# Attention with rope, two heads at a time: 128-row score products first, then the 64-row products of both heads in turns

## The chip, the core and the metric

One core of a Trainium2 chip runs the kernel. The metric is device time in microseconds (us). The kernel before took 2066.39 us, the median of three runs (2065.8 to 2067.51).

## What is computed

Two transformer blocks on 256 tokens of 2048 features, in float32. The first has sliding-window attention. The second has two attentions side by side, one with rope ("mla", 16 heads) and a differential one (8 heads), and a feed-forward layer. The change concerns the attention with rope, whose scores are a sum of two products: over 128 features of a head's own keys, and over 64 turned features whose keys all heads share.

```python
def mla_branch(c_q, c_kv, k_pe, ...):
    q = (rmsnorm_2(c_q, q_norm_g) @ w_uq).reshape(b, s, 16, 192)
    q_nope, q_rope = q[..., :128], apply_rope(q[..., 128:], cos, sin)
    kv = (rmsnorm_2(c_kv, kv_norm_g) @ w_ukv).reshape(b, s, 16, 256)
    k_nope, v = kv[..., :128], kv[..., 128:]
    k_rope = apply_rope(k_pe, cos, sin)                  # one for all heads
    # for each of the two blocks of 128 queries:
    sc = (einsum('bqhd,bkhd->bhqk', qn, k_nope) + einsum('bqhr,bkr->bhqk', qr, k_rope)) * scale
    sc = where(chunk_allowed(q_pos, k_pos), sc, -1e30)   # chunks of 64 tokens
    o = einsum('bhqk,bkhd->bqhd', softmax(sc), v)
```

No key of the second block of 128 is allowed to a query of the first. So a head has two score products: first queries with first keys (128 columns), second queries with all keys (256 columns).

## The kernel before

**Large matrices.** All weights lie in HBM as one run of 128x128 tiles in the order of use. SyncE's queue loads them 16 tiles at a time; half of that (8 tiles) at a time is split into an exact high part (`w_hi`, ScalarE, line 84) and a low part (`w_lo`, VectorE, line 85), with four buffers for each. A product with a tile is two instructions on TensorE, 512 columns with the high part and 256 with the low one, in `tile3`. Sums stand in four PSUM banks tagged `g`; from there ScalarE and VectorE take them (`total`, `scaled`, line 198 for the tensor-tensor operations, line 356 for the copy).

**Small work in between.** Attention is written as generators. `Interleave` (line 123) lets one of them go one step after every `every` tiles of weights, and a step of the same piece comes at the earliest `apart` steps later. In the part of interest `every` is 5 and `apart` is 4 (line 703). A planner then orders each engine's instructions by program order and by when it expects operands and buffers to be free, so that an instruction with a late operand may be passed by later ones.

**Attention with rope.** The loop at line 688 runs over four groups of four heads. A group makes its keys (`uk`, 4 x 4 tiles), its values (`uv`, 16 tiles, four at a time), its rope queries (`uq`, 2 x 6 tiles; two heads to a tile, each in one half of the 128 partitions) and its other queries (4 x 6 tiles). Behind the rope queries `rope_q` is queued, which turns them (`rotate`, line 618), and behind each head's queries `attend_m` (line 660), which waits until its group's queries are turned. Its three steps:
1. The scores into a bank tagged `s` (there are two). `scores` (line 363) does, in this order: 128 rows, 128 columns; 64 rows, 128 columns; 128 rows, 256 columns; 64 rows, 256 columns. All operands are float32, and the trace shows each product as two passes (a weight load and a matmul each). `exps` (line 371) takes the negated maximum on VectorE (line 375) and the exponential and its sum on ScalarE (line 379); the probabilities are then divided by the sum.
2. Three transposes into a bank tagged `t` (two of them), and a copy to SBUF on VectorE.
3. The products with the values, and the split of the result into `y_m`.

**Two other attentions** show in the trace what the change makes of this one. `attend_a` (line 442), in the first block, takes two heads at a time, whose 64 features lie in the two halves of the partitions; its products go in turns on the halves, into two `s` banks. `attend_d` (line 725) has two score sets of 128 rows in one step.

Of the kernel before, what the change touches and what calls it, by code (L numbers as in the profile page):

```python
# [10 lines left out]
F32R = mybir.dt.float32r  # L11
# [21 lines left out]
class Weights:  # L33
    """The weight matrices as one run of 128x128 tiles in the order of their use."""

# [19 lines left out]
    def pin(self, after, until):  # L55
        """Splits of tiles from `after` to `until`, counted from here, keep their place in the program."""
        i = len(self.order)
        self.pinned = range(i + after, i + until)

    def cut(self, i, parts=None):  # L60
        """The exact parts [hi], [lo] of half a chunk."""
        if i in self.halves:
            return
        nc = self.nc
        c = i // CH
        if c not in self.loaded:
            self.load(c)
        o = (i % CH) * P
        src = self.loaded[c][:, o:o + HALF * P]
        if o:  # L70
            self.loaded.pop(c)
        if parts is not None:
            self.halves[i] = parts
            for j, (hi, lo) in enumerate(parts):
                q = slice(j * HALF * P // 2, (j + 1) * HALF * P // 2)
                nc.scalar.copy(out=hi, in_=src[:, q])
                nc.vector.tensor_tensor(out=lo, in0=src[:, q], in1=hi.bitcast(F32), op=ALU.subtract)
            return
        hi = self.split.tile([P, HALF * P], F32R, name="w_hi", tag="w_hi", bufs=4)
        lo = self.split.tile([P, HALF * P], F32R, name="w_lo", tag="w_lo", bufs=4)  # L80
        n_cut = 2 if i < self.fine else 1
        for j in range(n_cut):
            q = slice(j * HALF * P // n_cut, (j + 1) * HALF * P // n_cut)
            a = nc.scalar.copy(out=hi[:, q], in_=src[:, q])  # L84
            b = nc.vector.tensor_tensor(out=lo[:, q], in0=src[:, q], in1=hi.bitcast(F32)[:, q], op=ALU.subtract)  # L85
            if i in self.pinned:
                self.tc.keep_in_program_order(a)
                self.tc.keep_in_program_order(b)
        self.halves[i] = [(hi, lo)]
# [16 lines left out]
class Lazy:  # L106
    """A list whose entries are made when they are first asked for, one ahead."""

# [14 lines left out]
class Interleave:  # L123
    """Pieces of work that go between the products of the large matrices, one step at a time.

    A piece is a generator; what it yields is the number of steps after which it goes on.
    """

# [39 lines left out]
def block_kernel(ctx, tc, order, w, xt, cols, bc, fg, cst, out):  # L168
# [30 lines left out]

# [1 line left out]
    ones = const.tile([P, P], F32, name="ones")  # L201
# [24 lines left out]

# [1 line left out]
    def split_scaled(src, g, hl):  # L228
        """hl = [hi | lo] of src * g, one factor per partition."""
        hi = hl[:, 0:S]  # L230
        if g is None:
            a = nc.scalar.copy(out=hi, in_=src)
            b = nc.vector.tensor_tensor(out=hl[:, S:], in0=src, in1=hi.bitcast(F32), op=ALU.subtract)
        else:
            a = nc.scalar.activation(out=hi, in_=src, func=AF.Copy, scale=g)
            b = nc.vector.scalar_tensor_tensor(out=hl[:, S:], in0=src, scalar=g, in1=hi.bitcast(F32),
                                               op0=ALU.mult, op1=ALU.subtract)
        return a, b

    class Squares:  # L240
        """Sums of squares over the features, for every token."""

# [37 lines left out]
    def rows(r, rb=None):  # L280
        """[any partition, token] = r[token, block], in PSUM, and in rb."""
        dg = unit("diag")[:, 0:S]
        for tb in range(2):
            nc.vector.tensor_scalar(out=dg[:, tb * P:tb * P + P], in0=ident, scalar1=r[:, tb:tb + 1], scalar2=None,  # L284
                                    op0=ALU.mult)
        ps = bank("t")
        mm(ps[:, 0:S], ones, dg, True, True)
        if rb is not None:
            nc.vector.tensor_copy(out=rb, in_=ps[:, 0:S])
        return ps[:, 0:S]  # L290

    def tile3(ps, name, row, col, hl, first, last):
        """One tile of weights against [hi | lo]: the product is the sum of the halves of ps."""
        hi, lo = W.take(name, row, col)
        mm(ps, hi, hl, first, False)
        mm(ps[:, 0:S], lo, hl[:, 0:S], False, last)
        between.tiles(1)

    def gemm(name, m, acts):
        """128 output features, transposed."""  # L300
        ps = bank("g")
# [5 lines left out]
    def gemm4(name, ms, acts):  # L307
        """As gemm, four at a time: for activations that come one by one."""
        pp = [bank("g"), bank("g"), bank("s"), bank("s")]
# [6 lines left out]
    def gemm_sum(name, m, acts):  # L316
        """As gemm, all products in one sum."""
        ps = bank("g")
# [9 lines left out]
    def blocks(name, m0, n, acts):  # L328
        """(block, bank) for n blocks, the first four by contraction."""
        for j, ps in enumerate(gemm4(name, range(m0, m0 + 4), acts)):  # L330
# [4 lines left out]
    def nat3(o, hl, tb, hi, lo, first, last):  # L335
        """Tokens as the stationary operand: o[token, feature]."""
        xh = hl[:, tb * P:tb * P + P]
# [5 lines left out]
    def gemm_nat(name, col, acts):  # L343
        """512 output features with the tokens in partitions: one bank for each block of tokens."""
        pp = [bank("g") for _ in range(2)]
# [8 lines left out]
    def total(o, ps):  # L354
        """The two halves of a product."""
        nc.scalar.copy(out=o, in_=ps[:, S:])
        tt(o, o, ps[:, 0:S], ALU.add)
# [5 lines left out]
    def scores(parts, ps):  # L363
        """ps[:, 0:128]: first queries, first keys; ps[:, 128:384]: second queries, all keys."""
        n = len(parts)
# [5 lines left out]
    def exps(ps, table, scale, negmax, sums, init):  # L371
        """exp(scale * (ps + table) - max) and its sums."""
        t = unit("prob")[:, 0:384]
# [9 lines left out]
    def transposed(p, on_act=False):  # L383
        """[keys, queries] of p: first keys (both blocks of queries), then second keys."""
        ps = bank("t")
# [8 lines left out]

    # ================= first block =================
    sq = Squares(8)
# [45 lines left out]
    def attend_a(j, q, o):  # L442
        """Heads a (an even group of keys) and b (an odd one), in the halves of the partitions."""
        kt = j // 8
# [41 lines left out]
    for j in range(16):  # L486
# [7 lines left out]
        for i, b in ((0, ps_0), (1, ps)) if j == 1 else ((j, ps),):  # L494
# [4 lines left out]
            between.add(attend_a(i, half(q, i), half(o, i)))  # L499
    # lambda, negated, in every partition  # L500
    lam = unit("lam")
# [72 lines left out]

    # ================= second block =================
    rope = unit("rope")
# [41 lines left out]
    def rotate(a):  # L618
        """Rope on a[:, 0:256] in place, both halves of the partitions alike."""
        ps = bank("t")  # L620
# [38 lines left out]

    def attend_m(head, qn, qr, kn, v):  # L660
        while head // 4 not in roped:
            yield
        negmax, sums, rec = sm("negmax"), sm("sums"), sm("rec")
        ps = bank("s")
        rng = slice(64 * (head % 2), 64 * (head % 2) + 64)
        scores([(qn, kn), (qr[rng], kr[rng])], ps)
        p = exps(ps, tab_m, scale_m, negmax, sums, BIG)
        nc.vector.reciprocal(out=rec[:, 0:2], in_=sums[:, 0:2])
        nc.scalar.activation(out=p[:, 0:P], in_=p[:, 0:P], func=AF.Copy, scale=rec[:, 0:1])
        nc.vector.tensor_scalar(out=p[:, P:384], in0=p[:, P:384], scalar1=rec[:, 1:2], scalar2=None, op0=ALU.mult)  # L670
        yield
        pt = transposed(p)
        yield
        ps = bank("t")
        mm(ps[:, 0:S], v[0], pt[:, 0:S], True, False)
        mm(ps[:, P:S], v[1], pt[:, S:384], False, True)
        y_m[head] = unit(f"y_m{head}", F32R)
        split_scaled(ps[:, 0:S], None, y_m[head])

# [8 lines left out]
    for u in range(4):  # L688
# [20 lines left out]
        for i in range(4):  # L709
            ps = gemm("uq", 4 * u + i, cq)  # L710
            if i % 2 == 0:
                qn.append(unit("q_n"))
            scaled(half(qn[-1], i), ps, rb_q)
            between.add(attend_m(4 * u + i, half(qn[-1], i), half(qr, i // 2), half(kn[i // 2], i),
                                 [t[:, i * P:i * P + P] for t in v]))

    # differential attention
    y_d = [None] * 16
# [117 lines left out]

    # residual, feed-forward
    sq = Squares(16)
# [127 lines left out]
def _matrices(i):  # L966
    """The weight matrices, their rows and columns in the order in which the kernel has the features."""
    pairs = []
# [60 lines left out]
```

## Time and profile before

| | |
|---|---|
| time, median of three runs | 2066.39 us |
| profiled execution: span, first to last instruction | 2065.4 us |
| TensorE (PE) busy | 2045.3 us, 99% |
| VectorE (DVE) busy | 1294.0 us, 63% |
| ScalarE (ACT) busy | 1057.7 us, 51% |
| chain that ended last | PE 98% |

The profile gives the profiled execution's own time only as its span; 1.0 us lies between that and the median of the runs. In the rows below, PE is TensorE's matmuls and PEld its weight loads, times are us from the span's start, and "L195" is line 195 (the helper that every matmul goes through, so groups are told apart by tile names: `ps_s<-k_n,q_n` are 128-row score products, `ps_s<-rb_kr,q_r` the 64-row ones). Matmuls overlap: the start of the next one tells more than the duration.

### The profile page before, as it was taken

The numbers are of one execution on the slowest core, as the hardware profiler recorded it, in microseconds if no ns is written. First come the engines' busy times: TensorE is split into PE (matmuls) and PEld (weight loads), VectorE is DVE, ScalarE is ACT, GpSimd is POOL, SyncE is SP. The second block draws the span as 40 slices with busy tenths as digits, with TensorE's granted clock in tenths as the row PEclk, the third lists the DMA queues.
The fourth block names the chain that finished last, engine by engine and source line by source line (L and its number), as shares of the span: only waits on it lengthen the run. The fifth ranks groups of instructions, "written<-read, shape, count | busy, mean of one in ns | idle before, by whom it ended". The sixth has DMA issues, their size and how long they took to land.

```text
span 2065.4 us, 28636 instructions
## 1 busy us (share of the span) xinstructions
PE 2045.3 (99%) x11290; PEld 1745.2 (84%) x11290; DVE 1294.0 (63%) x2145; ACT 1057.7 (51%) x1810; POOL 15.6 (1%) x25
## 2 busy tenths in 40 slices
PE   8999999999999999999999999999999999999998
PEld 7878888888888888888888888888888888888886
DVE  7768766877666555566565667655656555554443
ACT  6667555655545444455464445454444444444443
POOL 0000000000000000000000000000000000000000
PEclk9999999999999999999999999999999999999999
DMA  7433454443434555545545555555555555555552
GB/s 291 147 135 141 165 202 186 147 159 123 146 125 176 184 188 183 184 166 181 180 167 184 184 185 185 182 182 184 184 185 186 191 189 188 184 206 201 185 202 102
DMA packets 53670, 364.92 MB, mean 177 GB/s; under 512 B 6240, under 2 KB 7136, under 8 KB 10400
## 3 DMA queue, kind: packets, MB, share of 16 engines
q1 hardware_dynamic: 52560, 361.07, 48.9%
q8 instruction: 88, 1.44, 0.3%
q0 software_dynamic: 400, 1.31, 0.2%
q10 hardware_dynamic: 576, 0.72, 0.1%
q14 instruction: 46, 0.38, 0.1%
HBM read 360.98 MB, written 2.10 MB: 176 GB/s over the span
## 4 chain that ended last, share of the span: by engine, by line
PE 98%; DVE 1%; issue 0%; ACT 0%; DMA 0%; POOL 0%; SPq 0%; ACTq 0%; POOLq 0%
PE ps_g L195 89%; PE ps_s L195 5%; PE ps_t L195 2%; PE ps_t L387 1%; DVE w_lo L85 0%; DMA w_raw<-w 0%; ACT w_hi L84 0%; DVE prob L375 0%; PE ps_t L768 0%; PE ps_t L864 0%; PE ps_t L744 0%; POOL rstd L277 0%; DVE diag L284 0%; DVE prob L468 0%; DVE y L561 0%
## 5 line engine op out<-in xcount | busy, mean ns | idle before, releaser
L85 DVE TENSOR_TENSOR w_lo<-w_raw,w_hi 128x1024 fp32r<-128x1024 f32 (+1 forms) x676 | 825.2, 1221 | 649.2 <-ACT w_hi L84 644.9
L84 ACT CAST w_hi<-w_raw 128x1024 fp32r<-128x1024 f32 (+1 forms) x676 | 707.5, 1047 | 851.8 <-PE ps_g L195 598.1
L195 PE MATMUL ps_g<-h,w_hi 128*128 128x512 f32 x3064 | 1100.4, 402 | 6.5 <-ACT w_hi L84 6.5
L195 PE MATMUL ps_g<-h,w_lo 128*128 128x256 f32 x3064 | 861.2, 281 | 0.0
L195 PEld LDWEIGHTS ps_g<-h,w_hi 128*128 128x128 f32 x3064 | 576.4, 188 | 152.4 <-issue 7.4
L195 PEld LDWEIGHTS ps_g<-h,w_lo 128*128 128x128 f32 x3064 | 579.5, 189 | 1.4 <-DVE w_lo L85 0.4
L195 PE MATMUL ps_g<-w_hi,act 128*128 128x512 f32 x704 | 217.0, 389 | 0.0
L195 PEld LDWEIGHTS ps_g<-w_hi,act 128*128 128x128 f32 x704 | 132.1, 188 | 27.5
L195 PE MATMUL ps_g<-w_lo,act 128*128 128x512 f32 x352 | 136.9, 389 | 0.0
L195 PE MATMUL ps_g<-y_m,w_hi 128*128 128x512 f32 x256 | 91.4, 399 | 0.0
L195 PE MATMUL ps_g<-y_d,w_hi 128*128 128x512 f32 x256 | 90.5, 399 | 0.0
L195 PE MATMUL ps_g<-g,w_hi 128*128 128x512 f32 (+1 forms) x240 | 80.0, 383 | 0.0
L195 PE MATMUL ps_g<-mg,w_hi 128*128 128x512 f32 x224 | 79.9, 399 | 0.0
L195 PE MATMUL ps_g<-w_hi,h 128*128 128x512 f32 x256 | 79.5, 389 | 0.0
L195 PEld LDWEIGHTS ps_g<-w_lo,act 128*128 128x128 f32 x352 | 66.1, 188 | 13.7
L195 PE MATMUL ps_g<-c,w_hi 128*128 128x512 f32 x208 | 77.3, 410 | 0.0
L195 PE MATMUL ps_g<-y_d,w_lo 128*128 128x256 f32 x256 | 71.9, 281 | 0.0
L195 PE MATMUL ps_g<-y_m,w_lo 128*128 128x256 f32 x256 | 71.8, 281 | 0.0
L379 ACT ACTIVATE prob<-prob,negmax 128x128 f32<-128x128 f32 (+1 forms) x128 | 57.0, 447 | 23.2 <-DVE negmax L375 23.0
L195 PE MATMUL ps_g<-g,w_lo 128*128 128x256 f32 x224 | 63.0, 281 | 0.0
L195 PE MATMUL ps_g<-mg,w_lo 128*128 128x256 f32 x224 | 62.9, 281 | 0.0
L195 PE MATMUL ps_g<-c,w_lo 128*128 128x256 f32 x208 | 58.3, 280 | 0.0
(238 smaller groups left out, 2031.3 us busy)
## 6 DMA issues: line engine op xcount, KB each, us to landing
w_raw<-w SPq DMA_DIRECT2D x337, 1024.0 KB, 4.8
w_raw<-w SPq DMA_DIRECT2D x5, 512.0 KB, 8.2
out<-x2n SPq DMA_DIRECT2D x8, 256.0 KB, 3.1
x_t<-xt SPq DMA_DIRECT2D x7, 256.0 KB, 7.6
fgt<-fg POOLq DMA_DIRECT2D x4, 256.0 KB, 6.5
w_raw<-w SPq DMA_DIRECT2D x2, 256.0 KB, 4.3
x_t<-xt SPq DMA_DIRECT2D x2, 128.0 KB, 3.1
lam<-bc POOLq DMA_DIRECT2D x1, 256.0 KB, 4.7
```

What stands on the lines that cost most here:

```text
L84: a = nc.scalar.copy(out=hi[:, q], in_=src[:, q])
L85: b = nc.vector.tensor_tensor(out=lo[:, q], in0=src[:, q], in1=hi.bitcast(F32)[:, q], op=ALU.subtract)
L195: nc.tensor.matmul(out=o, lhsT=a, rhs=b, start=start, stop=stop, skip_group_check=True)
L379: nc.scalar.activation(out=t[:, a:b], in_=t[:, a:b], func=AF.Exp, scale=-1.0, bias=negmax[:, qb:qb + 1], accum_out=sums[:, qb:qb + 1])
L387: nc.tensor.transpose(out=ps[:, j * P:j * P + P], in_=p[:, j * P:j * P + P], identity=ident)
```

## The change

`attend_m` takes two heads. It asks for both `s` banks, does the 128-row products of the first head, then those of the second, and then the 64-row products: 128 columns of the first head (rows 0 to 63) and of the second (rows 64 to 127), then 256 columns of both. The reciprocal is taken once for a pair. The transposes of both heads are one step, and the copy of the second head's goes to ScalarE. The value products of both heads are one step, into one `t` bank. A pair is queued behind every second head's queries. Comments and docstrings elsewhere are emptied; line numbers stay nearly the same.

```diff
-    def attend_m(head, qn, qr, kn, v):
-        while head // 4 not in roped:
+    def attend_m(j, qn, qr, kn, v):
+
+        while j // 2 not in roped:
             yield
         negmax, sums, rec = sm("negmax"), sm("sums"), sm("rec")
-        ps = bank("s")
-        rng = slice(64 * (head % 2), 64 * (head % 2) + 64)
-        scores([(qn, kn), (qr[rng], kr[rng])], ps)
-        p = exps(ps, tab_m, scale_m, negmax, sums, BIG)
-        nc.vector.reciprocal(out=rec[:, 0:2], in_=sums[:, 0:2])
-        nc.scalar.activation(out=p[:, 0:P], in_=p[:, 0:P], func=AF.Copy, scale=rec[:, 0:1])
-        nc.vector.tensor_scalar(out=p[:, P:384], in0=p[:, P:384], scalar1=rec[:, 1:2], scalar2=None, op0=ALU.mult)
-        yield
-        pt = transposed(p)
+        pp = [bank("s") for _ in range(2)]
+        for e, ps in enumerate(pp):
+            mm(ps[:, 0:P], qn[e][:, 0:P], kn[e][:, 0:P], True, False)
+            mm(ps[:, P:384], qn[e][:, P:S], kn[e], False, False)
+        for a, b, n in ((0, P, P), (P, S, S)):
+            for e, ps in enumerate(pp):
+                rng = slice(64 * e, 64 * e + 64)
+                mm(ps[:, a:a + n], qr[rng, a:b], kr[rng, 0:n], False, a > 0)
+        p = [exps(ps, tab_m, scale_m, negmax[:, 2 * e:2 * e + 2], sums[:, 2 * e:2 * e + 2], BIG)
+             for e, ps in enumerate(pp)]
+        nc.vector.reciprocal(out=rec, in_=sums)
+        for e in range(2):
+            nc.scalar.activation(out=p[e][:, 0:P], in_=p[e][:, 0:P], func=AF.Copy, scale=rec[:, 2 * e:2 * e + 1])
+            nc.vector.tensor_scalar(out=p[e][:, P:384], in0=p[e][:, P:384], scalar1=rec[:, 2 * e + 1:2 * e + 2],
+                                    scalar2=None, op0=ALU.mult)
+        yield
+        pts = [transposed(p[e], e == 1) for e in range(2)]
         yield
         ps = bank("t")
-        mm(ps[:, 0:S], v[0], pt[:, 0:S], True, False)
-        mm(ps[:, P:S], v[1], pt[:, S:384], False, True)
-        y_m[head] = unit(f"y_m{head}", F32R)
-        split_scaled(ps[:, 0:S], None, y_m[head])
+        for e in range(2):
+            o = e * S
+            mm(ps[:, o:o + S], v[e][0], pts[e][:, 0:S], e == 0, False)
+            mm(ps[:, o + P:o + S], v[e][1], pts[e][:, S:384], False, e == 1)
+        for e in range(2):
+            y_m[2 * j + e] = unit(f"y_m{2 * j + e}", F32R)
+            split_scaled(half(ps, e), None, y_m[2 * j + e])
...
-            between.add(attend_m(4 * u + i, half(qn[-1], i), half(qr, i // 2), half(kn[i // 2], i),
-                                 [t[:, i * P:i * P + P] for t in v]))
+            if i % 2:
+                between.add(attend_m(2 * u + i // 2, [half(qn[-1], e) for e in range(2)], half(qr, i // 2),
+                                     [half(kn[i // 2], e) for e in range(2)],
+                                     [[t[:, e * P:e * P + P] for t in v] for e in (i - 1, i)]))
```

## Rows read from the trace of the kernel before

**Rows 1.** The page: span, busy time of the engines, chain that ended last by engine.
```profile
span 2065.4 us, 28636 instructions
PE 2045.3 (99%) x11290; PEld 1745.2 (84%) x11290; DVE 1294.0 (63%) x2145; ACT 1057.7 (51%) x1810; POOL 15.6 (1%) x25
...
PE 98%; DVE 1%; issue 0%; ACT 0%; DMA 0%; POOL 0%; SPq 0%; ACTq 0%; POOLq 0%
```

**Rows 2.** Waits of PE, longest in total first: us, times, longest.
```profile
PE ps_g L195 <- ACT w_hi L84: 6.5, 1, 6.5
```

**Rows 3.** Busy time by stretch: length, engines' busy us (instructions), clock, DMA share, GB/s.
```profile
430.00:616.00 186.00, 186.00 (x988) 151.91 (x987) 129.48 (x292) 94.84 (x195) 0.00 (x0) 1.00 0.39 137
...
447.40:465.00 17.60, 17.60 (x81) 12.61 (x80) 13.85 (x44) 9.52 (x27) 0.00 (x0) 1.00 0.31 120
```

**Rows 4.** Timeline of PE at the first head's scores: start us, us, instruction.
```profile
449.01 0.27 PE L195 MATMUL ps_g<-c,w_lo 128*128 128x256 f32 x1
449.12 0.38 PE L195 MATMUL ps_s<-k_n,q_n 128*128 128x128 f32 x2
...
450.48 0.70 PE L195 MATMUL ps_s<-rb_kr,q_r 64*128 64x256 f32 x2
...
451.44 0.28 PE L195 MATMUL ps_g<-c,w_lo 128*128 128x256 f32 x1
```

**Rows 5.** Timeline of PE at one pair of the first block's attention.
```profile
46.95 0.28 PE L195 MATMUL ps_g<-h,w_lo 128*128 128x256 f32 x1
47.16 0.93 PE L195 MATMUL ps_s<-k_a,q_a 64*128 64x128 f32 x8
...
48.36 0.28 PE L195 MATMUL ps_g<-h,w_lo 128*128 128x256 f32 x1
...
48.72 0.28 PE L195 MATMUL ps_g<-h,w_lo 128*128 128x256 f32 x1
```

**Rows 6.** Score products by tile: count, ns min/median/max, first and last start us.
```profile
L195 PE MATMUL ps_s<-k_n,q_n x64: 270/327/483, 449.1 to 593.7; 128*128 128x128 f32 x32, 128*128 128x256 f32 x32
...
L195 PE MATMUL ps_s<-rb_kr,q_r x64: 272/374/480, 449.4 to 594.3; 64*128 64x128 f32 x32, 64*128 64x256 f32 x32
```

**Rows 7.** Timeline of PE at two score sets of the differential attention.
```profile
638.64 0.28 PE L195 MATMUL ps_g<-h,w_lo 128*128 128x256 f32 x1
638.75 1.47 PE L195 MATMUL ps_s<-qk_d 128*128 128x128 f32 x8
...
640.30 0.28 PE L195 MATMUL ps_g<-h,w_lo 128*128 128x256 f32 x1
```

**Rows 8.** Timeline of PE at another pair of the first block's attention.
```profile
189.83 0.92 PE L195 MATMUL ps_s<-k_a,q_a 64*128 64x128 f32 x4
...
191.11 0.92 PE L195 MATMUL ps_s<-k_a,q_a 64*128 64x128 f32 x4
191.96 0.39 PE L195 MATMUL ps_g<-h,w_lo 128*128 128x256 f32 x1
```

**Rows 9.** Timeline of DVE behind the turning of the first group's queries.
```profile
449.42 0.42 DVE L198 TENSOR_TENSOR q_r<-q_r,rope_t 128x256 f32<-128x256 f32 x1
449.75 0.42 DVE L198 TENSOR_TENSOR q_n<-q_n,rb_lat 128x256 f32<-128x256 f32 x1
```

**Rows 10.** Timeline of all engines behind one pair of the first block.
```profile
80.75 0.93 PE L195 MATMUL ps_s<-k_a,q_a 64*128 64x128 f32 x8
...
81.81 0.35 DVE L375 CUSTOM_DVE_ANT_0 prob<-ps_s,bias,negsink 128x128 f32<-128x128 f32 x1 [2.60 <-ACT w_hi L84]
...
82.49 0.08 DVE L375 DVE_READ_ACCUMULATOR2_ANT negmax<- 128x1 f32 x1
...
83.17 0.08 DVE L375 DVE_READ_ACCUMULATOR2_ANT negmax<- 128x1 f32 x1
...
83.77 1.22 DVE L85 TENSOR_TENSOR w_lo<-w_raw,w_hi 128x1024 fp32r<-128x1024 f32 x1
...
85.69 0.70 ACT L467 ACTIVATE prob<-prob,rec 128x128 f32<-128x128 f32 x2
```

## Prediction

> **What bounds the kernel now.** I read the page first: span, busy line, chain. TensorE is busy for 99% of the span and the chain that ended last runs over it for 98% [rows 1]. The list of its waits is the second view: one wait of 6.5 us, for the first weights, is the longest [rows 2]. So a microsecond taken from TensorE's queue comes off the span, unless something else is then late. The third view is the busy time by stretch: in the attention with rope (430 to 616 us) TensorE is busy for all 186 us, VectorE for 129.48, ScalarE for 94.84, and the clock is granted in full [rows 3]. Where the scores of the first four heads lie (447.4 to 465) VectorE is busy for 13.85 of 17.6 us; it is the engine to watch.
>
> The time of before in the runs is 2066.39 us; the profiled execution has a span of 2065.4, so 1.0 us lies around it. The sum is made on the span and carried over.
>
> **What it removes: the switches.** Between large products TensorE does one head's scores: a 128-row product of 128 columns, a 64-row one, a 128-row one of 256 columns, a 64-row one, each in two passes. The timeline shows what a head takes [rows 4]: from the start of the last weight product before it (449.01) to the start of the first such product behind the next large one (451.44) are 2.43 us. Without a head, one such step of a large product takes 0.35 us (48.36 to 48.72 is 0.36 [rows 5]). A head so costs 2.08 us, and a pair, with no switch saved between its two heads, 4.16. There are 64 passes of either kind [rows 6], that is 16 heads with four of each, or eight pairs.
>
> **What it adds.** The new order does both heads' 128-row products, then the four 64-row products in turns on the halves of the rows. Both parts stand in the trace of before, in other attentions.
> - The 128-row part: the differential attention does two score sets of 128 rows, 8 passes, with no switch. From 638.64 to 640.30 are 1.66 us [rows 7]; less 0.35, 1.31 us a pair. That is also what 16 heads' 128-row work amounts to, so nothing else hides in it.
> - The 64-row part: the first block's attention does exactly these four products, of the same columns, two heads in turns on rows 0 to 63 and 64 to 127, each into a bank of its own. From 46.95 to 48.36 are 1.41 us [rows 5]; less 0.35, 1.06 us with the switch in and the switch out.
>
> A pair takes 1.31 + 1.06 = 2.37 us, where it took 4.16. That is 1.79 us a pair, 14.3 us for eight.
>
> Do the 64-row products run beside each other? Eight passes of two heads took 0.93 us from first start to last end [rows 5]; four passes of one head alone, at 189.83, took 0.92 [rows 8]. So the second head is free in the trace. The Trainium skill speaks against a factor of two: "TensorE: Matmul & The Clock Gate", in the section on measured speedup against the span model, gives 3.07 for four row tiles, 77% of the ideal. By that, as an estimate, two tiles would win a factor of 1.5, each pair would keep some 0.2 us more, and the time would be 1.6 us longer. The rows are of the same products, so I go by them.
>
> **What it moves.** The three steps of a head (scores, transposes, values) become three steps of a pair. `Interleave` gives a step after five tiles of weights, after eight where tiles come by fours, and a group of four heads has 16 + 16 + 12 + 24 = 68 tiles, about 13 steps. Before, a group wanted two steps of rope and 4 x 3 of heads, more than there were, and the heads ran late (the last 64-row pass starts at 594.3 [rows 6], far into the next matrix). After it wants 2 + 2 x 3 = 8. Counting the tiles through the code puts the scores of the pairs at tiles 73, 78, 151, 164, 214, 219, 277 and 287, and each pair's transposes at least 20 tiles behind. TensorE's work is the same wherever it stands, so the earlier place is worth nothing by itself. Transposes and value products are the same in number and shape: nothing. The reciprocal of four columns in place of two of two, and half the copies of the transposed probabilities moved from VectorE to ScalarE, lie under TensorE: both engines have room over the stretch [rows 3], and with it gone they would cost a part of what VectorE already does there. No DMA is added or moved, none passes another on SP's or POOL's queue, and weights keep their buffers.
>
> **What the new order waits for.** Three waits can come up; behind each stand the next large products on TensorE, so what is not covered is lost.
> - The pair at tile 73 follows its own last queries. Today the last multiply of these ends at 449.75 + 0.42 = 450.17 [rows 9], and its second head would start at 449.12 + 0.65 = 449.77 (half of 1.31 behind the first). 0.4 us late, at the first group; none if the planner moves a large product ahead, 1.22 if a split is put in front, and I take the 0.4. The last group has the same order, with longer tiles behind it, and is taken at none. The turned queries are nearer: done at 449.42 + 0.42 = 449.84 [rows 9], wanted 1.31 behind the start, at 450.43.
> - A pair wants both score banks, and there are two. VectorE's minimum has read the first head's bank at 82.57 and the second's at 83.25, when the products ended at 80.75 + 0.93 = 81.68 [rows 10]: 0.9 and 1.6 us. Five tiles are 1.75 us, and the second head's bank is wanted 0.65 later: covered by 0.8 us. One `w_lo` split in front of the minimum (1.22 us [rows 10]) leaves 0.4. This close following occurs twice (73 and 78, 214 and 219). Between none and 1.22 us each; I take 0.4 each, since VectorE's 13.85 us in the first stretch [rows 3] would meet 17.6 less 2 x 1.79 = 14.0 us.
> - The transposes want the pair's probabilities. In the first block's pairs they are done at 85.69 + 0.70 = 86.39 [rows 10], 4.7 us behind the products; here 20 tiles, 7.0 us, lie between. Covered.
>
> Together 0.4 + 2 x 0.4 = 1.2 us. The sum is 14.3 - 1.2 = 13.1 us: a span of 2052.3, and a time of 2066.39 - 13.1 = 2053.3 us.
>
> **Rivals.**
> - *The two heads don't run beside each other.* When a bank or an operand is late, the planner puts a large product between the two heads: that has happened to one pair of the first block, at 189.83 and 191.11 [rows 8]. Each head then pays the whole 64-row part. A pair costs 1.31 + 2 x 1.06 = 3.43 and wins 0.73; eight win 5.8, 2060.6 us. For it: banks and queries are as near as worked out above. Against: it was one pair there, with pairs following each other as closely as the closest here. One or two such pairs cost about 1 us each and stay in the forecast's own range.
> - *VectorE becomes the bound where the scores lie.* Both banks come free later, and every pair waits for one `w_lo` in front of the minimum, 1.22 x 8 = 9.8 us: the gain is 4.5, 2061.9 us. This is also what the Trainium skill warns of ("TensorEngine Tiling (Array Packing)", section PSUM Bottleneck: tiling speeds up TensorE but not the emptying of PSUM). For it: the 14.0 us against 13.85 of the first group. Against: the weights are split up to four halves ahead, and in only one other group do the pairs follow each other as closely, so that a delay has time to go away.
> - *Slower: the transposes wait.* They stand at the head of TensorE's queue, and the normalisation of two heads now has to be done before the first of them. It decides from a chain over 7.0 + 1.79 = 8.8 us. At 9.5 us each pair loses 2.5 and wins 1.79, 5.7 us slower in all: 2072 us. The chain in the trace is 4.7 us, so more than three splits would have to get in front of it at all eight pairs.
>
> **How the numbers follow.** Forecast 0.76, with its own range from 2051 (no wait, a little more won than worked out) to 2056 (two pairs split and a wait each); heads not beside each other 0.10; VectorE 0.09; slower 0.03; something else, of either sign, 0.02. The range for 8 in 10 goes from 2050.8 to 2059.5: below lies a gain that no row supports, above the worse ends of the two middle cases. A change of under 0.2% (4.1 us) can't be told from none here. The first three cases are over that except for the worst of VectorE's: faster 0.92, same 0.04, slower 0.04.
>
> **What would show it.** In the profile after: the products of 128 rows of both heads together, then eight 64-row passes in some 0.9 us, eight times; a pair's cost at 2.4 us by the same reading; TensorE's waits in the stretch under 2 us in all; the large products unchanged, and about 13 us off the span. A large product between two heads' 64-row passes speaks for the first rival, waits of the score products on the minimum for the second, waits of the transposes on the probabilities for the third. The forecast is wrong if the pair costs over 3 us, or if TensorE waits for over 4 us.

## The result

The changed kernel takes 2053.01 us, the median of four runs (2052.82 to 2053.45); the kernel before took 2066.36 beside it (2065.8 to 2067.51). The ratio is 0.9934, with a 95% interval from 0.9922 to 0.9946: 13.4 us less, where 13.1 had been forecast.

### The profile page after: what moved, and what is told of

Read it like the earlier page. It is cut to its first block, busy times and chain, and to the rows that moved or that the text cites. A ratio compares the mean times of both kernels' runs of the same rounds, so it can differ in the third digit from the quotient of the medians.

```text
span 2051.0 us, 28625 instructions
## 1 busy us (share of the span) xinstructions
PE 2030.9 (99%) x11290; PEld 1738.8 (85%) x11290; DVE 1289.2 (63%) x2129; ACT 1057.6 (52%) x1818; POOL 15.6 (1%) x25
## 3 DMA queue, kind: packets, MB, share of 16 engines
q0 software_dynamic: 400, 1.31, 0.2%
## 4 chain that ended last, share of the span: by engine, by line
PE 98%; DVE 1%; issue 0%; ACT 0%; DMA 0%; POOL 0%; SPq 0%; ACTq 0%; POOLq 0%
PE ps_g L195 90%; PE ps_s L195 5%; PE ps_t L195 2%; PE ps_t L387 1%; DMA w_raw<-w 0%; DVE prob L375 0%; DVE w_lo L85 0%; PE ps_t L782 0%; PE ps_t L878 0%; ACT w_hi L84 0%; PE ps_t L758 0%; POOL rstd L277 0%; DVE prob L468 0%; DVE y L561 0%; DVE y L560 0%
## 5 line engine op out<-in xcount | busy, mean ns | idle before, releaser
L195 PEld LDWEIGHTS ps_g<-y_d,w_hi 128*128 128x128 f32 x256 | 48.1, 188 | 12.1
```

What stands on the lines that cost most here:

```text
L195: nc.tensor.matmul(out=o, lhsT=a, rhs=b, start=start, stop=stop, skip_group_check=True)
```

## The profile after

The page of the changed kernel: TensorE is still the bound, at 99%, and over the same large products. It has lost 14.4 us of busy time and the span 14.4 us [rows 1].

```profile
span 2051.0 us, 28625 instructions
PE 2030.9 (99%) x11290; PEld 1738.8 (85%) x11290; DVE 1289.2 (63%) x2129; ACT 1057.6 (52%) x1818; POOL 15.6 (1%) x25
...
PE 98%; DVE 1%; issue 0%; ACT 0%; DMA 0%; POOL 0%; SPq 0%; ACTq 0%; POOLq 0%
```

Busy time by stretch (columns as in [rows 3]): the attention with rope, now 430 to 602 us, has no gap on TensorE, and VectorE is busy for 123.47 of 172 us; around the first two pairs (446.2 to 460.2) for 11.5 of 14.

```profile
430.00:602.00 172.00, 172.00 (x985) 145.90 (x984) 123.47 (x272) 95.41 (x203) 0.00 (x0) 1.00 0.42 148
446.20:460.20 14.00, 14.00 (x79) 10.93 (x78) 11.50 (x40) 8.97 (x27) 0.00 (x0) 1.00 0.21 76
```

The list of waits, for the same part of the run (430 to 610): TensorE's matmuls have none. Its weight loads have these three lines (us in total, times, longest):

```profile
PEld ps_g L195 <- issue: 2.7, 8, 0.3
PEld ps_s L195 <- issue: 2.3, 7, 0.3
PEld ps_s L195 <- DVE q_r L198: 1.3, 4, 0.3
```

These are gaps of 0.33 us, found where the products change between 128 and 64 rows; before, the list has some 30 of them in this part, now 19. The four put down to the turned queries (`q_r`) are no longer than the others, and the first of these queries were ready before they were wanted (448.65 against 448.91). No line names the minimum (`negmax`), which empties the score banks, or the probabilities.

The timeline of PE at the second pair that runs. By the same reading as in [rows 4], from the large product before (452.54) to the one behind the next (455.25) are 2.71 us; less 0.35, a pair costs 2.36 us. Eight passes of 128 rows and eight of 64 stand together.

```profile
452.54 0.28 PE L195 MATMUL ps_g<-c,w_lo 128*128 128x256 f32 x1
452.66 1.47 PE L195 MATMUL ps_s<-k_n,q_n 128*128 128x128 f32 x8
454.06 0.93 PE L195 MATMUL ps_s<-rb_kr,q_r 64*128 64x128 f32 x8
...
455.25 0.28 PE L195 MATMUL ps_g<-c,w_lo 128*128 128x256 f32 x1
```

Six of the eight pairs look like this. Two do not. The first pair that runs in the last group has its heads one after the other, with four switches and no rows beside each other: 548.07 to 551.82, 3.75 - 0.35 = 3.40 us.

```profile
548.07 0.28 PE L195 MATMUL ps_g<-h,w_lo 128*128 128x256 f32 x1
548.19 0.82 PE L195 MATMUL ps_s<-k_n,q_n 128*128 128x128 f32 x4
548.94 0.92 PE L195 MATMUL ps_s<-rb_kr,q_r 64*128 64x128 f32 x4
549.79 0.92 PE L195 MATMUL ps_s<-k_n,q_n 128*128 128x128 f32 x4
550.64 0.92 PE L195 MATMUL ps_s<-rb_kr,q_r 64*128 64x128 f32 x4
...
551.82 0.28 PE L195 MATMUL ps_g<-h,w_lo 128*128 128x256 f32 x1
```

And the first pair that runs in the first group has a large product and a first pair of 64-row passes ahead of the second head's 128-row products. From 447.82 to 451.25 are 3.43 us; the large product in between and the step at the end take 0.47 (0.35, and 0.12 from a low part to the next high one, 451.48 to 451.60), so the pair costs 2.96 us.

```profile
447.82 0.27 PE L195 MATMUL ps_g<-c,w_lo 128*128 128x256 f32 x1
447.94 0.81 PE L195 MATMUL ps_s<-k_n,q_n 128*128 128x128 f32 x4
448.40 0.58 PE L195 MATMUL ps_g<-c,w_hi 128*128 128x512 f32 x1
448.91 0.49 PE L195 MATMUL ps_s<-rb_kr,q_r 64*128 64x128 f32 x2
449.33 0.92 PE L195 MATMUL ps_s<-k_n,q_n 128*128 128x128 f32 x4
450.18 0.92 PE L195 MATMUL ps_s<-rb_kr,q_r 64*128 64x128 f32 x6
...
451.25 0.39 PE L195 MATMUL ps_g<-c,w_hi 128*128 128x512 f32 x1
451.48 0.28 PE L195 MATMUL ps_g<-c,w_lo 128*128 128x256 f32 x1
451.60 0.40 PE L195 MATMUL ps_g<-c,w_hi 128*128 128x512 f32 x1
```

Sum: 16 x 2.08 = 33.3 us before ([rows 4]; the trace shows the same at the other heads), 6 x 2.36 + 2.96 + 3.40 = 20.5 after: 12.8 us of the gain are the score products. The spans of the two profiles differ by more, 14.4 us. Of that, 1.2 us lie ahead of the first score product (447.82 here, 449.01 in [rows 4]), where the change does nothing; in e1 below, which leaves the heads alone, this point lies at 448.37, so it moves from kernel to kernel, and I count none of it for the change. The median moved by 13.4, since 1.8 us lie around this profile's span (2052.82 - 2051.0) and 1.0 around that of before. So some half a microsecond of the gain is not put down to anything. Most of it lies in the same part of the run: the large products are the same in the same order, and the one that starts at 614.12 us before starts at 599.79 after. These are 14.3 us, 13.1 of them behind the first score product, so 0.4 us there are not score products.

## Experiments

The theory: the gain has two parts, fewer switches between 128 and 64 rows, and the second head's 64-row products beside the first's; waits take nothing, and what is lost is lost by the planner's order at two pairs. Rivals: only one of the two parts wins; the copy that went to ScalarE helps; VectorE or the normalisation nearly became the bound.

| kernel | us, median | less than before |
|---|---|---|
| changed | 2053.01 | 13.4 |
| e1_one_head | 2060.36 | 6.4 |
| e2_same_half | 2058.11 | 8.6 |
| e3_not_in_turns | 2053.52 | 13.2 |
| e4_pinned | 2051.45 | 15.3 |
| e5_apart1 | 2057.35 | 9.9 |
| e6_vector_2 | 2053.89 | 13.4 |
| e7_vector_6 | 2056.16 | 11.1 |
| e8_copies_vector | 2052.83 | 14.5 |
| e9_pinned_both | 2051.68 | 15.0 |
| e10_three_times | 2074.22 | -7.5 |

The kernel before beside them had medians of 2066.36 to 2067.28; each row is taken against its own.

**e1_one_head: the switches alone.** In the kernel before, `scores`:

```diff
         for j, (q, k) in enumerate(parts):
             mm(ps[:, 0:P], q[:, 0:P], k[:, 0:P], j == 0, False)
-        for j, (q, k) in enumerate(parts):
             mm(ps[:, P:384], q[:, P:S], k[:, 0:S], False, j == n - 1)
```

> The kernel before (one head at a time), with both 128-row products of a head ahead of both 64-row ones. It keeps the switches of a head from four to two and leaves the heads alone. Theory (a switch has a price of its own, and the rest of the gain is the running beside each other): a head takes 0.655 + 1.06 = 1.72 us in place of 2.08, 16 heads win 5.9 us, about 2060.5 us. Rival (only the running beside each other wins; a switch costs nothing that the longer products don't hide): no change, 2066.4 us. Second rival (the switches are all of it): a gain near the whole change's 13.4 us, 2053 us.

It took 2060.36 us, 6.4 less than before; ratio 0.9969 (0.9957 to 0.9981). A head takes 2.05 - 0.35 = 1.70 us (448.37 to 450.42) where it took 2.08.

```profile
448.37 0.27 PE L195 MATMUL ps_g<-c,w_lo 128*128 128x256 f32 x1
448.48 0.82 PE L195 MATMUL ps_s<-k_n,q_n 128*128 128x128 f32 x4
449.23 0.92 PE L195 MATMUL ps_s<-rb_kr,q_r 64*128 64x128 f32 x4
...
450.42 0.28 PE L195 MATMUL ps_g<-c,w_lo 128*128 128x256 f32 x1
```

As the theory had it (1.72 us, 2060.5 us). Two switches fewer are worth 0.38 us a head, 0.19 each on the mean. This part of the gain, nearly half, needs no pairs at all.

**e2_same_half: the rows alone.** In the changed kernel:

```diff
-                rng = slice(64 * e, 64 * e + 64)
+                rng = slice(0, 64)
```

> The changed kernel, but the second head's 64-row products read rows 0 to 63 too, the first head's rope queries (so its scores are another sum). Instructions, shapes and order are the same. Theory (the second head's products are free because they stand on the other half of the rows): each of the six pairs whose products go in turns pays the second head's four passes again, 0.64 us, and the pair at the start some 0.4: 6 x 0.64 + 0.4 = 4.3 us more, 2057.3 us, and a pair's score products take 3.0 us in place of 2.36. Rival (fewer switches is all that wins; the halves don't matter): 2053.0 us and 2.36 us a pair.

It took 2058.11 us. The order of the instructions is the same on every engine, and a pair takes 3.36 - 0.35 = 3.01 us (453.14 to 456.50): eight 64-row passes are spread over 1.57 us, where they took 0.93.

```profile
453.14 0.28 PE L195 MATMUL ps_g<-c,w_lo 128*128 128x256 f32 x1
...
454.66 1.57 PE L195 MATMUL ps_s<-rb_kr,q_r 64*128 64x128 f32 x8
...
456.50 0.28 PE L195 MATMUL ps_g<-c,w_lo 128*128 128x256 f32 x1
```

The theory held, and the rival is out. The second head is free because it stands on the other half of the rows, 0.65 us a pair. With the switches the pair's gain is accounted for: six fewer of 0.19 and the 0.65 are 1.79 us, and 4.16 - 2.36 are 1.80. The time is 5.1 us longer, of which 6 x 0.65 and some 0.4 at the first pair are seen in the score products; the rest was not looked for.

**e3_not_in_turns: is the turn-taking needed?**

```diff
-        for a, b, n in ((0, P, P), (P, S, S)):
-            for e, ps in enumerate(pp):
+        for e, ps in enumerate(pp):
+            for a, b, n in ((0, P, P), (P, S, S)):
                 rng = slice(64 * e, 64 * e + 64)
```

> The changed kernel, but the 64-row products of the first head both come ahead of those of the second, not in turns. Theory (TensorE starts products in the order given, and a product waits for the one before it on its own half alone): the second head's first pass can start only beside the first head's last one, so three of its four passes are no longer hidden, 0.43 us a pair; for six pairs 2.6 us, 2055.6 us, a pair at 2.79. Rival (the order doesn't matter as long as the halves differ): 2053.0 us. Second rival (nothing runs beside anything unless it goes in turns): 0.64 a pair, 2056.9 us.

My theory failed: it took 2053.52 us, within 0.5 of the changed kernel, and a pair is the same 2.71 - 0.35 = 2.36 us. All four passes of the first head are written ahead of the second's, the planner leaves that order (the program that it makes has the four on rows 0 to 63 ahead of the four on rows 64 to 127), and the eight still take 0.93 us together. Four passes of one head alone take 0.92 us [rows 8], so the second head's must have started beside them, ahead of passes written before them.

```profile
452.62 0.28 PE L195 MATMUL ps_g<-c,w_lo 128*128 128x256 f32 x1
...
454.14 0.93 PE L195 MATMUL ps_s<-rb_kr,q_r 64*128 64x128 f32 x8
...
455.33 0.28 PE L195 MATMUL ps_g<-c,w_lo 128*128 128x256 f32 x1
```

**e10_three_times: how far ahead?** As e3, with the 64-row products of each head three times over:

```diff
+            for i in range(3):
                 for a, b, n in ((0, P, P), (P, S, S)):
                     rng = slice(64 * e, 64 * e + 64)
-                    mm(ps[:, a:a + n], qr[rng, a:b], kr[rng, 0:n], False, a > 0)
+                    mm(ps[:, a:a + n], qr[rng, a:b], kr[rng, 0:n], False, i == 2 and a > 0)
```

> The changed kernel with all 64-row products of the first head ahead of all of the second, and each done three times into the same sum (so the scores hold the rope part three times): 12 passes of one half ahead of 12 of the other, where four ahead of four had run beside each other. Theory (a product waits only for those on its own half, however many of the other half are written ahead of it): the second half's first pass starts some 10 to 40 ns behind the first half's; a pair takes 1.31 + 3 x 0.64 + 0.42 = 3.65 us. Rival (TensorE looks only some four passes ahead): the second half starts some 8 passes, 1.28 us, late, and a pair takes 4.9 us.

My theory (3.65 us) failed, and the rival (4.9) is near: a pair takes 5.09 us (455.17 to 460.61 are 5.44). By stretch, for the instructions on the rope queries alone: in the first 1.41 us TensorE starts 8 passes, and the other 16 (with one that reaches over) lie in the following 2.15.

```profile
455.17 0.28 PE L195 MATMUL ps_g<-c,w_lo 128*128 128x256 f32 x1
...
456.69 3.65 PE L195 MATMUL ps_s<-rb_kr,q_r 64*128 64x128 f32 x24
...
460.61 0.28 PE L195 MATMUL ps_g<-c,w_lo 128*128 128x256 f32 x1
```
```profile
456.69:458.10 1.41, 1.41 (x8) 1.30 (x9) 0.00 (x0) 0.00 (x0) 1.00 0.00 0
458.12:460.27 2.15, 2.15 (x17) 1.70 (x15) 0.00 (x0) 0.00 (x0) 1.00 0.00 0
```

So the second half starts beside the ninth pass of twelve: it overtakes four passes (two products) and not twelve. With the kernel's four passes a head the written order doesn't matter. With longer runs it does; how they would fare in turns was not run.

**e4_pinned: the planner's order.** The changed kernel, with the products of a pair kept in their order:

```diff
-            mm(ps[:, 0:P], qn[e][:, 0:P], kn[e][:, 0:P], True, False)
+            pin(mm(ps[:, 0:P], qn[e][:, 0:P], kn[e][:, 0:P], True, False))
...
-                mm(ps[:, a:a + n], qr[rng, a:b], kr[rng, 0:n], False, a > 0)
+                pin(mm(ps[:, a:a + n], qr[rng, a:b], kr[rng, 0:n], False, a > 0))
```

(`mm` returns the instruction, and the second 128-row product is pinned alike.)

> The changed kernel with the eight score products of a pair kept in their written order, so that the planner no longer takes the two pairs apart that it did (the first of the first group, at 448 us, and the first of the last group, at 548 us). Theory (the planner's order lost 0.6 us at the one and 1.04 at the other, and the operand that it thought late is there in time): all eight pairs at 2.36 us, 1.6 us less, 2051.4 us. Rival (the planner was right: the second head's queries are late, and TensorE now waits for them as long as it had lost): 2053.0 us, with a wait of some 0.4 to 1 us in front of the second head's first product at these two places.

It took 2051.45 us, ratio 0.9927 (0.9914 to 0.9939), the fastest of all. The order differs from the changed kernel's in these two places alone. The planner now puts a whole large product between the two heads' 128-row products, where it costs nothing, and keeps the 64-row ones together. At the last group, 547.27 to 550.33 are 3.06 us, less two steps of 0.35: 2.36, where it was 3.40. TensorE waits for nothing there.

The number of the theory came out, but its reason doesn't follow: the large product stands where the wait would have been. Without it the second head would have been due 0.65 us behind the first, at 547.39 + 0.65 = 548.04, and the last multiply of its queries ends at 548.21 (VectorE: 547.80 + 0.41). So they would have been late, as the rival had it. The large product covers that and costs nothing, where the changed kernel's order cost 1.04 us.

```profile
547.27 0.28 PE L195 MATMUL ps_g<-h,w_lo 128*128 128x256 f32 x1
547.39 0.82 PE L195 MATMUL ps_s<-k_n,q_n 128*128 128x128 f32 x4
547.85 0.58 PE L195 MATMUL ps_g<-h,w_hi 128*128 128x512 f32 x1
548.27 0.28 PE L195 MATMUL ps_g<-h,w_lo 128*128 128x256 f32 x1
548.39 0.82 PE L195 MATMUL ps_s<-k_n,q_n 128*128 128x128 f32 x4
549.14 0.93 PE L195 MATMUL ps_s<-rb_kr,q_r 64*128 64x128 f32 x8
...
550.33 0.28 PE L195 MATMUL ps_g<-h,w_lo 128*128 128x256 f32 x1
```

**e9_pinned_both.** The same `pin` on the products of the first block's pairs as well.

> The changed kernel with the order kept in both places: the eight score products of a rope pair, and the four of a pair of the first block, where the planner had taken one pair apart (at 189.83 us before). There the kept order leaves the first head's first product alone and the other three together. Theory (order is all that is lost): 0.4 to 0.6 us less than with the rope pairs alone, 2051.0 us. Rival (the second bank is late there, and TensorE now waits for it): 2051.5 us or up to 0.5 more, with a wait on the minimum in front of the second head's product.

It took 2051.68 us (2051.61 to 2052.92), not to be told from e4's 2051.45 (2050.99 to 2052.42). Inconclusive in the time. In the trace the first block's pair does get shorter, by 0.43 us, as the theory had it: 1.67 us (190.17 to 192.89, less three steps of 0.35) where e4 has 2.10 (188.84 to 191.41, less 0.47 for a step and a low part). The profiled execution is longer than e4's all the same, 2050.5 against 2049.2 us. It had lost 1.3 us before 25 us, 0.4 of it in the first wait for weights (6.9 us, where e4 has 6.5): scatter of that size hides the gain.

**e5_apart1: what keeps the transposes from waiting?**

```diff
-            between.every, between.apart = 5, 4
+            between.every, between.apart = 5, 1
```

> The changed kernel, but the steps of a piece follow each other after one step of the interleaving in place of four (apart 1 in place of 4): a pair's transposes are written 5 tiles, 1.75 us, behind its scores, where 20 tiles, 7.0 us, were. The chain from the products to the probabilities is some 4.7 us. Theory (the planner covers a late operand by moving large products ahead): within 3 us of the changed kernel, 2053 to 2056 us. Rival (the written distance is what covers it; it is what kept the third rival of the prediction away): about 3 us of waiting for each of eight pairs, 2077 us, with TensorE waiting for the probabilities.

It took 2057.35 us, 4.3 more than the changed kernel (3.5 by what each is less than before): far from the 24 us of waits, a little over the bound of my theory. By the list of waits, TensorE's weight loads lost 2.0 us in all to the probabilities and 0.9 to their copies, eight and three times; its matmuls have no wait in the list.

```profile
PEld ps_t L387 <- ACT prob L677: 2.0, 8, 0.3
PEld ps_t L195 <- ACT prob_t L390: 0.9, 3, 0.4
```

The rest is order. Large products were moved in front of the transposes: those of the pair below start at 451.46, 3.6 us behind the pair's end (447.87), where 1.75 had been written. And the first pair of every group now comes apart (the timeline, large products left out):

```profile
442.93 0.81 PE L195 MATMUL ps_s<-k_n,q_n 128*128 128x128 f32 x4
443.67 0.92 PE L195 MATMUL ps_s<-rb_kr,q_r 64*128 64x128 f32 x4
...
446.28 0.81 PE L195 MATMUL ps_s<-k_n,q_n 128*128 128x128 f32 x4
447.02 0.92 PE L195 MATMUL ps_s<-rb_kr,q_r 64*128 64x128 f32 x4
```

Here the second head starts 3.35 us behind the first, and each has its 64-row passes by itself: 2 x 1.70 = 3.40 us a pair. Four such pairs against 3.40, 2.96 and two of 2.36 in the changed kernel are 2.5 us more, most of the loss. So the planner keeps the transposes from waiting, and pairs lose their running side by side. What it took these pairs apart for was not read.

**e6_vector_2 and e7_vector_6: VectorE.** Ahead of each pair's minimum, two or six more multiplies:

```diff
+        for _ in range(2):
+            tt(unit("load"), rope, rope, ALU.mult)
         p = [exps(ps, tab_m, scale_m,
```

> The changed kernel, with two more multiplies of 128x512 on VectorE ahead of each pair's minimum (about 0.75 us each by twice the 128x256 one, 1.5 us a pair, 12 us in all), whose results nothing reads. Theory (VectorE's spare time and the order of the planner cover what is put in front of the minimum): within 1 us of 2053.0. Rival (VectorE bounds the stretch with the scores, the second rival of the prediction): the two closest pairs wait 1 us each, or, where every pair is as tight, 8 x 1 us: 2055 to 2061 us, and TensorE's score products wait for the minimum.

> As the one with two, but six multiplies ahead of each pair's minimum, 4.5 us a pair, 36 us in all. VectorE is busy for some 125 of 172 us of the stretch, so that 47 us are spare. Theory (covered as long as the sum fits): the sum still fits, but not beside each pair's scores: 2 to 8 us more than 2053.0. Rival (what counts is the stretch at the scores alone, where nothing is spare): most of the 4.5 us of every pair shows, 28 to 36 us more, 2081 to 2089 us. Second rival (VectorE covers it all): 2053 us.

Each multiply took 0.68 us, so 1.4 and 4.1 us a pair, 11 and 33 us in all. The times are 2053.89 and 2056.16, 13.4 and 11.1 less than before where the changed kernel is 13.4 less: nothing, and 2.3 us, as both theories had it. With two no wait came up in the stretch on the score products' banks. With six the matmuls have 0.8 us of waits, none of them on a score bank, and the list has, among others, these waits of TensorE's weight loads that the changed kernel's has not:

```profile
PEld ps_g L195 <- DVE w_lo L85: 1.4, 3, 0.9
...
PEld ps_s L195 <- DVE negmax L375: 0.4, 1, 0.4
```

So less than a tenth of 33 us shows. VectorE had room for all of the pairs' work, and where it runs out it is mostly the weights' low parts that come late, and the banks hardly.

**e8_copies_vector: the copies undone.**

```diff
-        pts = [transposed(p[e], e == 1) for e in range(2)]
+        pts = [transposed(p[e]) for e in range(2)]
```

> The changed kernel with one part undone: the transposed probabilities of both heads are copied on VectorE, as before, not those of the second on ScalarE. TensorE's instructions are the same. Theory (the gain is all in the score products): 2053.0 us, within 0.5. Rival (the copy on ScalarE carries part of the gain, by freeing VectorE): 1 to 3 us more.

2052.83 us, 0.2 less than the changed kernel; against the kernel before beside each it is 1.1 less (14.5 and 13.4), but the spans of the two profiles are 2051.2 and 2051.0. No loss either way: the rival's 1 to 3 us more are out, and this part of the change is worth nothing that shows.

## Why the prediction was right, point by point

- **A pair at 2.37 us in place of 4.16** (1.79 a pair): right for six pairs, 2.36. The two prices read off the other attentions, 1.31 and 1.06 [rows 5, 7], hold here. e1 and e2 split them: about 0.76 of a pair's 1.8 us are the switches inside the heads (e1), the rest the switches between the heads and the other half of the rows (0.65, e2).
- **The total, 13.1 against 13.4**: so near in part by luck. The score products gave 12.8, and some half a microsecond came from elsewhere, not put down to anything.
- **Beside each other, by a factor of two**: right; e2 against the changed kernel is the full 0.65. The estimate from the Trainium skill's packing figure ("TensorE: Matmul & The Clock Gate", Measured speedup vs the span model) would have left 0.2 us a pair; the trace does not agree with it for two halves.
- **Waits of 1.2 us**: the size was near, 1.6 us, but not what it was made of. That the second head's queries are late was right. In the changed kernel the multiply that finishes them ends at 448.57 + 0.41 = 448.98 at the first group. The first head's products start at 447.94, so the second's were due 0.65 later, at 448.59: 0.39 late, where I took 0.4. At the last group, which I took at none, it is 549.01 against 548.19 + 0.65 = 548.84, 0.17 late.

```profile
448.57 0.41 DVE L198 TENSOR_TENSOR q_n<-q_n,rb_lat 128x256 f32<-128x256 f32 x1
...
548.60 0.41 DVE L198 TENSOR_TENSOR q_n<-q_n,rb_lat 128x256 f32<-128x256 f32 x1
```

Wrong was what becomes of it. I had a wait, or a large product moved ahead that costs nothing. The planner put 64-row passes of the first head into the gap (at the first group behind a high part of a large product), and so took the pair apart: 0.60 us lost for 0.39 late, 1.04 for 0.17, the loss of the first rival at two pairs. I had one or two such pairs in the forecast's own range. e4 has the large product in that place, and nothing is lost. That the planner did this because of the late queries is argued, and why it chose the dear filling was not tested.

- **Bank waits of 0.4 at the two close places**: did not occur; no wait in the list names the minimum. e6 shows that there was room for more.
- **VectorE and the transposes as rivals**: neither shows in the list of waits after, and e7 and e5, which leave them less room, cost no more than 2.3 and 3.5 us.
- **Nothing for copies, reciprocals, places**: right for the copies (e8). The others were not run by themselves; the half microsecond without an owner is all that is left for them.

## What to carry to other kernels

A price for a new order of products can often be read off the same trace, where another part of the kernel already does it; measure from the large product before to the one behind it, not by durations. Group products of the same row tiling first, since that needs no pairing and was here nearly half of the gain; then put the small products on both halves of the rows. And look at the order that the planner made: an operand that was 0.2 to 0.4 us late cost 0.6 and 1.0 us, with 64-row passes put in the gap, and keeping the pair's order gave another 1.6 us.

## What the runs showed of the hardware

- A switch between 128 and 64 rows costs 0.19 us of TensorE on the mean (e1: 0.38 us for two).
- Products on different halves of the rows start out of their written order: passes of the second half overtook four passes of the first (e3), and of twelve only the last four ran beside them (e10). "TensorE: Matmul & The Clock Gate" of the Trainium skill, in the section "The mechanism", says that matmuls start and end in strict order; these two runs show otherwise for the starts on two halves.
